# Weights split into high and low halves: two separate tiles, or one tile in which the halves alternate

## The chip, the core and the metric

One core of one Trainium2 chip runs the whole program. The metric is device time in microseconds, the median of three runs. The profile is of one further execution.

## The reference

A streaming encoder trunk of two layers with D = 2048 and 288 tokens: 256 of a prompt and 32 of a sample stream, which share all weights. Every token goes through the same weight products; the mixers in between work on chunks.

```
layer 0:  x += out_ab( retention(h) || gated linear attention(h) )      h = rmsnorm(x)
          x += convffn(rmsnorm(x))
layer 1:  x += out_att( chunked band attention with bias(h) )           h = rmsnorm(x)
          x += convffn(rmsnorm(x))
y = rmsnorm(x)

convffn(h):  g, u = split(h @ w_up);  act = silu(causal conv3(g) + b) * u;  return act @ w_down      (D_FF = 5632)
```

All inputs, weights and outputs are float32. Beside y the program returns the recurrent states, the new keys and values, and the last gate rows of the convolutions.

## The kernel before, in words

Activations lie transposed: 128 features on the partitions, 288 tokens along the row. A 128-row piece of the model dimension is one tile row of 288 float32, that is 1152 bytes. Every weight product is a sum of matmuls of a 128x128 weight block (stationary) with such a row (moving). To keep float32 accuracy with the float32r form of the matmul, both operands are split into a high half, rounded to float32r, and a low half, the rest; each block is multiplied three times: high by high, high by low, low by high (`passes`, L83 to L85). The three matmuls each load their weights anew, so the high weights are loaded twice running.

`project` (L65) makes one output tile of 128 features: it walks over 16 or 22 blocks in chunks of up to 8 (`WCH`). For each chunk `weights` (L54) issues one DMA of 512 KB on SP's queue into `w` (four buffers), lets ACT cast it into `wh` (L61) and DVE subtract into `wl` (L62), three buffers each. The tile framework places the waits: a cast waits until PE has read the buffer that it reuses.

The moving operands are constants for the whole program: `xh`, `xl` (the normed input of a layer) and `bh`, `bl` (the input of an output projection or of the down product). Before the change the two halves of piece k lie side by side in one tile `x{k}` of 2304 bytes, and likewise in `b`. The further rows that the down product needs (k from 16 to 21) are tiles of the same form in the FFN's own pool (`ffn`, L290).

Stages in order: `start` computes the first products straight from a packed input `x_first`, in pieces given by `cuts` (L92), while the data arrives; `ab_mixer` runs eight heads in an order written out by `chain`; `out_proj` (L277) adds its products to the residual `x`, which is loaded anew from DRAM by four DMAs on SP's queue just ahead of it (L219, L220), because its place served as mixer storage until then; then FFN, attention, out_proj, FFN. SP's queue carries the weights in program order. POOL's queue carries small loads, states and outputs. Padding in some constant tiles (`ones`, `w2`, `x`) moves what is allocated behind them.

The functions that the diff touches follow.

Of the kernel before, what the change touches and what calls it, by code (L numbers as in the profile page):

```python
# [5 lines left out]
F32 = mybir.dt.float32  # L6
# [6 lines left out]
P = 128  # L13
# [24 lines left out]
class Trunk:  # L38
# [15 lines left out]
    def weights(self, src, n, lo=False):  # L54

        nc = self.nc
        w = self.wp.tile([P, WCH, P], F32, name="w", tag="w", bufs=4)[:, :n, :]
        h = self.wp.tile([P, WCH, P], F32R, name="wh", tag="wh", bufs=3)[:, :n, :]
        l = self.wp.tile([P, WCH, P], F32R, name="wl", tag="wl", bufs=3)[:, :n, :]
        nc.sync.dma_start(w, src)  # L60
        nc.scalar.copy(h, w)  # L61
        nc.vector.tensor_tensor(l, w, h.bitcast(F32), op=ALU.subtract)  # L62
        return h, l

    def project(self, src, xh, xl, nk, k0=0, chunks=None, part=None, ps=None):  # L65
# [21 lines left out]
    def first_products(self, src, xw, lo_h):  # L87


        nc = self.nc  # L90
        ps = [self.acc_ps.tile([P, 512], F32, name="acc", tag="acc")[:, :T] for _ in range(N_FIRST + 1)]
        cuts = (0, 1, 2, 3, 4, 6, 8, 10, 12, 14, 16)  # L92

        for _ in range(8):
            nc.tensor.matmul(self.mm()[:, :P], lhsT=self.ones, rhs=self.ones, start=True, stop=True)
        for c, (i, j) in enumerate(zip(cuts, cuts[1:])):
            n = j - i
            nc.sync.dma_start(xw[:, i:j, :], src[:, i:j, :])
            w = xw[:, i:j, T : T + N_FIRST * P].rearrange("p k (o m) -> p k o m", o=N_FIRST)
            wlo = xw[:, i:j, T + N_FIRST * P :]  # L100
            lo = lo_h[:, i:j, :]
            tile = lambda tag: self.wp.tile([P, WCH, P], F32R, name=tag, tag=tag, bufs=3)[
                :, : N_FIRST * n, :
            ].rearrange("p (k o) m -> p k o m", o=N_FIRST)
            h, l = tile("wh"), tile("wl")
            for k in range(i, j):
                self.gain_in(k, 0)
                if k == i:
                    if c:
                        nc.scalar.copy(h, w)  # L110
                    else:
                        nc.vector.tensor_copy(h, w)
                    nc.vector.tensor_tensor(l, w, h.bitcast(F32), op=ALU.subtract)
                    nc.gpsimd.tensor_copy(lo[:, :, :RANK], wlo)
                    nc.gpsimd.tensor_tensor(
                        lo[:, :, RANK : 2 * RANK], wlo, lo[:, :, :RANK].bitcast(F32), op=ALU.subtract
                    )
                first, last = k == 0, k == KD - 1
                at = k - i
                for o in range(N_FIRST):  # L120
                    nc.tensor.matmul(ps[o], lhsT=h[:, at, o, :], rhs=self.xh[k], start=first, stop=False)
                for o in range(N_FIRST):
                    nc.tensor.matmul(ps[o], lhsT=h[:, at, o, :], rhs=self.xl[k], start=False, stop=False)
                for o in range(N_FIRST):
                    nc.tensor.matmul(ps[o], lhsT=l[:, at, o, :], rhs=self.xh[k], start=False, stop=last)
                nc.tensor.matmul(ps[-1], lhsT=lo[:, at, :], rhs=self.xh[k], start=first, stop=False)
                nc.tensor.matmul(ps[-1], lhsT=lo[:, at, :], rhs=self.xl[k], start=False, stop=last)
        return ps
# [67 lines left out]
    def run(self, ctx):  # L196
        nc, a = self.nc, self.a

        ones = self.const("ones", [P, P + 32])
        self.ones, self.eps = ones[:, :P], ones[:, P : P + 1]  # L200
        xs = [self.const(f"x{k}", [P, 2, T], F32R) for k in range(KD)]
        self.xh, self.xl = [[x[:, i, :] for x in xs] for i in range(2)]
        b_all = self.const("b", [P, KD, 2, T], F32R)
        self.bh_all, self.bl_all = b_all[:, :, 0, :], b_all[:, :, 1, :]
        self.bh, self.bl = [[b_all[:, k, i, :] for k in range(KD)] for i in range(2)]
        self.R = self.const("R", [P, T])
        nc.vector.memset(self.ones, 1.0)
# [7 lines left out]
        with self.tc.tile_pool(name="x", bufs=1) as xp:  # L215

            x = xp.tile([P, KD * T + 16], F32, name="x", tag="x")[:, : KD * T].rearrange("p (k t) -> p k t", t=T)
            self.x = [x[:, k, :] for k in range(KD)]
            for k in range(0, KD, 4):  # L219
                nc.sync.dma_start(x[:, k : k + 4, :], a["xT"][:, k : k + 4, :])  # L220
            self.out_proj(a["w_out_ab"], 1, (WCH, 0))
            with self.tc.tile_pool(name="f0", bufs=2) as pool:
# [27 lines left out]
    def start(self, pool):  # L250
# [14 lines left out]

        self.w2 = self.const("w2", [P, 512 + 224])[: 2 * RANK + 1, :512]
        nc.sync.dma_start(self.w2, a["w2"])
# [8 lines left out]

    def out_proj(self, w, n, chunks):  # L277

        for m in range(KD):
            if m < len(self.started):  # L280
                ps = self.project(w[m], self.bh, self.bl, KD, chunks=chunks, part=1, ps=self.started[m])
            else:
                ps = self.project(w[m], self.bh, self.bl, KD, chunks=chunks)
            self.nc.vector.tensor_tensor(self.x[m], self.x[m], ps, op=ALU.add)
            self.norm_in(m, n)
        self.norm_stat()

    def ffn(self, pool, layer, n, x_all):
        nc, a = self.nc, self.a
        bs = [self._one(pool, f"b{k}", [P, 2, T], None, F32R) for k in range(KD, HALF)]  # L290
        bh, bl = [old + [b[:, i, :] for b in bs] for i, old in ((0, self.bh), (1, self.bl))]
        convp = self._one(pool, "convp", [P, NF, 4], a["convp"][:, layer])
# [74 lines left out]
    def head_out(self, pool, o, gates, hd, g):  # L367

        nc = self.nc
        sq = pool.tile([P, TP], F32, name="hsq", tag="hsq", bufs=1)  # L370
        sq2 = pool.tile([P, TP], F32, name="hsq2", tag="hsq2", bufs=1)
        nc.scalar.activation(sq, o[0], AF.Square)
# [94 lines left out]
    def ab_mixer(self, pool, k0, q0, v0, lo_ps, second):  # L467
# [38 lines left out]
        def ret(hd):  # L506
            if hd == 0:
                late["cos"], late["sin"] = one("cosR", [P, T], a["cos"]), one("sinR", [P, T], a["sin"])
                for t in late.values():
                    nc.gpsimd.tensor_tensor(t, t, self.R, op=ALU.mult)  # L510
# [16 lines left out]
    def gla_head(self, pool, hd, w, sums, masks, eyem, hg, s4, sts, first):  # L527
# [13 lines left out]
        z = [gate(0)] if first else []  # L541
        st = pool.tile([P, 256], F32, name="gst", tag="gst", bufs=GRP)
        nc.gpsimd.dma_start(st, a["state_gla"][hd])
        sts.append(st)

# [163 lines left out]
    def ret_head(self, pool, hd, w, cosR, sinR, kdec, hg, s4, sts, aside):  # L709
        nc, a = self.nc, self.a  # L710
        dec = pool.tile([P, 384], F32, name="dec", tag="dec")
        nc.gpsimd.dma_start(dec, a["dec"][hd])
        st = pool.tile([P, 2, 256], F32, name="rst", tag="rst", bufs=GRP)
        nc.gpsimd.dma_start(st, a["state_ret"][hd])
        sts.append(st.rearrange("p j v -> p (j v)"))

# [179 lines left out]
    def att_sample(self, pool, g, kept, v4, bd):  # L896
# [15 lines left out]
        s = pool.tile([P, T], F32, name="as4", tag="as4")  # L912
        own = pool.tile([P, GRP, TS], F32, name="own4", tag="own4")
        mx = pool.tile([P, 1], F32, name="mx4", tag="mx4")
# [22 lines left out]
        for i in range(2):  # L937
            for c, (_, _, vc) in zip(quarter, kept):
                nc.tensor.matmul(
                    po[c], lhsT=pT[:, 1 + i, c], rhs=vc[:, i, :], start=False, stop=i == 1, skip_group_check=True  # L940
                )
        o = pool.tile([P, P], F32, name="ao4", tag="ao4")
        nc.vector.tensor_scalar(o, po, sm, None, op0=ALU.mult)
# [141 lines left out]
```

## Time and profile before

| what | value |
| --- | --- |
| median of 3 runs | 2677.33 us (2676.45 to 2679.82) |
| profiled execution, its own time | 2679.3 us |
| its span, first to last instruction | 2677.2 us |
| PE, DVE, ACT, POOL busy | 99%, 58%, 42%, 5% |
| matmuls | 20079 |
| mean DMA rate | 167 GB/s |

The span is what the trace covers; the 2.1 us beside it lie outside the first and last instruction. PE is the matmul side of TensorE, PEld its weight loads, which overlap the matmuls. A matmul's duration overlaps the next one's, so durations don't add up to time; distances between starts do.

### The profile page before, as it was taken

The numbers are of one execution on the slowest core, as the hardware profiler recorded it, in microseconds if no ns is written. First come the engines' busy times: TensorE is split into PE (matmuls) and PEld (weight loads), VectorE is DVE, ScalarE is ACT, GpSimd is POOL, SyncE is SP. The second block draws the span as 40 slices with busy tenths as digits, with TensorE's granted clock in tenths as the row PEclk, the third lists the DMA queues.
The fourth block names the chain that finished last, engine by engine and source line by source line (L and its number), as shares of the span: only waits on it lengthen the run. The fifth ranks groups of instructions, "written<-read, shape, count | busy, mean of one in ns | idle before, by whom it ended". The sixth has DMA issues, their size and how long they took to land. (4 is left out here: it accounts for less than half of the span.)

```text
span 2677.2 us, 48712 instructions
## 1 busy us (share of the span) xinstructions
PE 2661.0 (99%) x20079; PEld 2642.5 (99%) x20079; DVE 1560.8 (58%) x2593; ACT 1126.1 (42%) x1511; POOL 132.8 (5%) x459
## 2 busy tenths in 40 slices
PE   9999999999999999999999999999999999999998
PEld 9999999999999999999999999999999999999998
DVE  8665555566664456665555555556666545666544
ACT  7564445443333333334444443444333333333443
POOL 3000000000000000000021110000000000000000
PEclk9999999999999999999999999999999999999999
DMA  6444445555555555555565565555555555555554
GB/s 230 151 138 156 157 157 193 167 164 166 166 166 164 167 168 167 165 168 160 166 213 179 178 183 166 158 166 165 166 166 166 163 167 168 166 166 166 165 166 131
DMA packets 127227, 448.27 MB, mean 167 GB/s; under 512 B 16059, under 2 KB 16379, under 8 KB 127004
## 3 DMA queue, kind: packets, MB, share of 16 engines
q1 hardware_dynamic: 119852, 426.83, 51.5%
q0 software_dynamic: 7008, 18.29, 2.2%
q8 instruction: 157, 2.57, 0.4%
q14 instruction: 66, 0.54, 0.1%
q10 hardware_dynamic: 144, 0.04, 0.0%
HBM read 434.69 MB, written 10.40 MB: 166 GB/s over the span
## 5 line engine op out<-in xcount | busy, mean ns | idle before, releaser
L61 ACT CAST wh<-w 128x1024 fp32r<-128x1024 f32 (+1 forms) x812 | 839.2, 1034 | 1461.0 <-PE acc L84 1210.8
L62 DVE TENSOR_TENSOR wl<-w,wh 128x1024 fp32r<-128x1024 f32 (+1 forms) x812 | 976.4, 1203 | 738.4 <-ACT wh L61 737.4
L83 PE MATMUL acc<-x,wh 128*128 128x288 f32 x4432 | 1314.6, 297 | 0.0
L84 PE MATMUL acc<-x,wh 128*128 128x288 f32 x4432 | 1311.8, 296 | 0.0
L85 PE MATMUL acc<-x,wl 128*128 128x288 f32 x4432 | 1308.4, 295 | 0.0
L85 PEld LDWEIGHTS acc<-x,wl 128*128 128x128 f32 x4432 | 839.5, 189 | 0.3
L83 PEld LDWEIGHTS acc<-x,wh 128*128 128x128 f32 x4432 | 833.0, 188 | 1.6 <-issue 1.1
L84 PEld LDWEIGHTS acc<-x,wh 128*128 128x128 f32 x4432 | 833.3, 188 | 0.3
L83 PE MATMUL acc<-b,wh 128*128 128x288 f32 x1920 | 567.4, 296 | 0.5 <-ACT wh L61 0.5
L85 PE MATMUL acc<-b,wl 128*128 128x288 f32 x1920 | 566.2, 295 | 0.7 <-DVE wl L62 0.7
L84 PE MATMUL acc<-b,wh 128*128 128x288 f32 x1920 | 566.9, 295 | 0.0
L85 PEld LDWEIGHTS acc<-b,wl 128*128 128x128 f32 x1920 | 363.2, 189 | 1.2 <-DVE wl L62 1.0
L83 PEld LDWEIGHTS acc<-b,wh 128*128 128x128 f32 x1920 | 360.6, 188 | 1.3 <-ACT wh L61 1.1
L84 PEld LDWEIGHTS acc<-b,wh 128*128 128x128 f32 x1920 | 360.8, 188 | 0.1
L316 DVE SCALAR_TENSOR_TENSOR gc<-gp,convp,gc 128x290 f32<-128x290 f32 x176 | 91.2, 518 | 3.1
L322 DVE TENSOR_TENSOR v<-acc,R 128x288 f32<-128x288 f32 x88 | 40.3, 458 | 88.6 <-PE acc L85 88.6
L307 DVE TENSOR_TENSOR gp<-acc,R 128x256 f32<-128x256 f32 x88 | 37.4, 425 | 90.3 <-PE acc L85 90.1
L309 POOL COPY conv_out<-gp 128x2 f32<-128x2 f32 x88 | 16.4, 187 | 1309.3 <-DVE gp L307 1309.3
L147 ACT CAST b<-v 128x288 fp32r<-128x288 f32 x88 | 38.2, 434 | 16.1 <-DVE v L324 16.1
L323 DVE TENSOR_TENSOR v<-v,sg 128x256 f32<-128x256 f32 x88 | 37.4, 426 | 10.6 <-DVE v L322 1.8
L314 DVE TENSOR_SCALAR gc<-gp,convp 128x290 f32<-128x290 f32 x88 | 38.0, 431 | 9.4
L332 DVE TENSOR_TENSOR x<-x,acc 128x288 f32<-128x288 f32 x64 | 29.1, 454 | 19.2 <-PE acc L85 19.2
(301 smaller groups left out, 1140.1 us busy)
## 6 DMA issues: line engine op xcount, KB each, us to landing
w<-in_w_ffn_up SPq DMA_DIRECT2D x352, 512.0 KB, 3.7
w<-in_w_ffn_down SPq DMA_DIRECT2D x128, 512.0 KB, 3.7
w<-in_w_in SPq DMA_DIRECT2D x108, 512.0 KB, 3.8
w<-in_w_qkv SPq DMA_DIRECT2D x96, 512.0 KB, 3.8
w<-in_w_ffn_down SPq DMA_DIRECT2D x64, 384.0 KB, 3.2
w<-in_w_out_ab SPq DMA_DIRECT2D x32, 512.0 KB, 3.9
w<-in_w_out_att SPq DMA_DIRECT2D x32, 512.0 KB, 3.7
xw<-in_x_first SPq DMA_DIRECT2D x6, 560.0 KB, 7.9
```

Source lines behind the costliest of these rows:

```text
L61: nc.scalar.copy(h, w)
L62: nc.vector.tensor_tensor(l, w, h.bitcast(F32), op=ALU.subtract)
L83: nc.tensor.matmul(ps, lhsT=h, rhs=xh, start=first, stop=False)
L84: nc.tensor.matmul(ps, lhsT=h, rhs=xl, start=False, stop=False)
L85: nc.tensor.matmul(ps, lhsT=l, rhs=xh, start=False, stop=last)
L147: self.nc.scalar.copy(h, v)
L307: nc.vector.tensor_tensor(gp[:, 2 : TP + 2], g[:, :TP], self.R[:, :TP], op=ALU.mult)
L314: nc.vector.tensor_scalar(gc, gp[:, 0:W], cw[:, 0:1], cw[:, 3:4], op0=ALU.mult, op1=ALU.add)
L316: nc.vector.scalar_tensor_tensor(gc, gp[:, w : w + W], cw[:, w : w + 1], gc, op0=ALU.mult, op1=ALU.add)
L322: nc.vector.tensor_tensor(v, u, self.R, op=ALU.mult)
L323: nc.vector.tensor_tensor(v[:, :TP], v[:, :TP], s[:, :TP], op=ALU.mult)
L332: nc.vector.tensor_tensor(self.x[m], self.x[m], ps, op=ALU.add)
```

## The change

Four things change. The high and low half of a weight chunk go into one tile `whl` of twice the size in which they alternate element by element: `h` and `l` are views with a step of two elements, written so by ACT and DVE and read so by the weight loads. The moving operands become rows of 1152 bytes each, first all high rows, then all low rows, placed first in the constant pool. The residual is loaded in eight pieces of two rows on POOL's queue from within `out_proj`; from the third on, a one-element copy from a row that has just been added comes first, so that a piece goes out after that addition. The first products take the first eight rows one by one. Further, some tiles of the mixer and of attention share buffers or have fewer, and a padding shrinks.

```
 def weights(...):
-        h = self.wp.tile([P, WCH, P], F32R, name="wh", tag="wh", bufs=3)[:, :n, :]
-        l = self.wp.tile([P, WCH, P], F32R, name="wl", tag="wl", bufs=3)[:, :n, :]
+        h, l = self.split_weights(n)
...
+    def split_weights(self, n):
+        t = self.wp.tile([P, WCH, P, 2], F32R, name="whl", tag="whl", bufs=3)
+        return t[:, :n, :, 0], t[:, :n, :, 1]
...
-        cuts = (0, 1, 2, 3, 4, 6, 8, 10, 12, 14, 16)
+        cuts = (0, 1, 2, 3, 4, 5, 6, 7, 8, 10, 12, 14, 16)
...
-            tile = lambda tag: self.wp.tile([P, WCH, P], F32R, name=tag, tag=tag, bufs=3)[
-                :, : N_FIRST * n, :
-            ].rearrange("p (k o) m -> p k o m", o=N_FIRST)
-            h, l = tile("wh"), tile("wl")
+            h, l = [x.rearrange("p (k o) m -> p k o m", o=N_FIRST) for x in self.split_weights(N_FIRST * n)]
...
+        self.xh, self.xl = [[self.const(f"x{h}{k}", [P, T], F32R) for k in range(KD)] for h in "hl"]
+        self.bh_all, self.bl_all = [self.const(f"b{h}", [P, KD, T], F32R) for h in "hl"]
+        self.bh, self.bl = [[b[:, k, :] for k in range(KD)] for b in (self.bh_all, self.bl_all)]
+        self.R = self.const("R", [P, T])
         ones = self.const("ones", [P, P + 32])
-        xs = [self.const(f"x{k}", [P, 2, T], F32R) for k in range(KD)]
-        self.xh, self.xl = [[x[:, i, :] for x in xs] for i in range(2)]
-        b_all = self.const("b", [P, KD, 2, T], F32R)
-        self.bh_all, self.bl_all = b_all[:, :, 0, :], b_all[:, :, 1, :]
-        self.bh, self.bl = [[b_all[:, k, i, :] for k in range(KD)] for i in range(2)]
-        self.R = self.const("R", [P, T])
...
-            for k in range(0, KD, 4):
-                nc.sync.dma_start(x[:, k : k + 4, :], a["xT"][:, k : k + 4, :])
-            self.out_proj(a["w_out_ab"], 1, (WCH, 0))
+            self.out_proj(a["w_out_ab"], 1, (WCH, 0), x)
...
-        self.w2 = self.const("w2", [P, 512 + 224])[: 2 * RANK + 1, :512]
+        self.w2 = self.const("w2", [P, 512 + 32])[: 2 * RANK + 1, :512]
...
 def out_proj(self, w, n, chunks, load=None):
+        def piece(k, n):
+            nc.gpsimd.dma_start(load[:, k : k + n, :], self.a["xT"][:, k : k + n, :])
+        if load is not None:
+            piece(0, 2)
+            piece(2, 2)
         for m in range(KD):
...
+            k = 2 * m + 4
+            if load is not None and k < KD:
+                nc.vector.tensor_copy(load[:, k : k + 2, :1], load[:, m : m + 1, :1].to_broadcast([P, 2, 1]))
+                piece(k, 2)
             self.norm_in(m, n)
...
 def ffn(...):
-        bs = [self._one(pool, f"b{k}", [P, 2, T], None, F32R) for k in range(KD, HALF)]
-        bh, bl = [old + [b[:, i, :] for b in bs] for i, old in ((0, self.bh), (1, self.bl))]
+        bh, bl = [
+            old + [self._one(pool, f"b{h}{k}", [P, T], None, F32R) for k in range(KD, HALF)]
+            for h, old in (("h", self.bh), ("l", self.bl))
+        ]
...
-        sq2 = pool.tile([P, TP], F32, name="hsq2", tag="hsq2", bufs=1)
+        sq2 = pool.tile([P, TP], F32, name="on", tag="on", bufs=2)
...
-                late["cos"], late["sin"] = one("cosR", [P, T], a["cos"]), one("sinR", [P, T], a["sin"])
-                for t in late.values():
+                late["cos"], late["sin"] = [pool.tile([P, T], F32, name="sp", tag="sp", bufs=2) for _ in range(2)]
+                for x, t in late.items():
+                    nc.gpsimd.dma_start(t, a[x])
...
-        st = pool.tile([P, 256], F32, name="gst", tag="gst", bufs=GRP)
+        st = pool.tile([P, 512], F32, name="st", tag="st", bufs=GRP) if hd % 2 == 0 else None
+        sts += [st[:, :256], st[:, 256:]] if hd % 2 == 0 else []
...
-        st = pool.tile([P, 2, 256], F32, name="rst", tag="rst", bufs=GRP)
+        st = pool.tile([P, 512], F32, name="st", tag="st", bufs=GRP)
...
-        own = pool.tile([P, GRP, TS], F32, name="own4", tag="own4")
+        own = pool.tile([P, GRP, TS], F32, name="own4", tag="own4", bufs=1)
...
-        o = pool.tile([P, P], F32, name="ao4", tag="ao4")
+        o = pool.tile([P, P], F32, name="ao4", tag="ao4", bufs=1)
```

## Rows read from the trace of the kernel before

**Rows 1.** The page: engines' busy time, and the clock by slice

```profile
PE 2661.0 (99%) x20079; PEld 2642.5 (99%) x20079; DVE 1560.8 (58%) x2593; ACT 1126.1 (42%) x1511; POOL 132.8 (5%) x459
PEclk9999999999999999999999999999999999999999
```

**Rows 2.** Waits: who waited for whom, us in total, times, longest

```profile
PE mm L95 <- DVE ones L208: 1.1, 1, 1.1
...
ACT wh L61 <- PE acc L84: 1210.8, 633, 3.8
...
SPq L220 <- DMA out_ret_out<-rst: 6.4, 3, 5.3
```

**Rows 3.** The page's groups by line: busy us, mean ns of one

```profile
L61 ACT CAST wh<-w 128x1024 fp32r<-128x1024 f32 (+1 forms) x812 | 839.2, 1034 | 1461.0 <-PE acc L84 1210.8
L62 DVE TENSOR_TENSOR wl<-w,wh 128x1024 fp32r<-128x1024 f32 (+1 forms) x812 | 976.4, 1203 | 738.4 <-ACT wh L61 737.4
L83 PE MATMUL acc<-x,wh 128*128 128x288 f32 x4432 | 1314.6, 297 | 0.0
...
L85 PE MATMUL acc<-b,wl 128*128 128x288 f32 x1920 | 566.2, 295 | 0.7 <-DVE wl L62 0.7
```

**Rows 4.** Windows in both FFNs: length, busy time and counts, clock, DMA share, GB/s

```profile
840.00:960.00 120.00, 120.00 (x907) 120.00 (x906) 53.80 (x56) 40.26 (x41) 0.00 (x0) 1.00 0.60 169
980.00:1240.00 260.00, 260.00 (x1963) 260.00 (x1962) 162.63 (x266) 102.03 (x123) 9.89 (x58) 1.00 0.54 166
```

**Rows 5.** Timeline of PE, twelve steps of the float32r form: start, duration

```profile
1099.77 0.29 PE L83 MATMUL acc<-x,wh 128*128 128x288 f32 x1
...
1101.36 0.30 PE L83 MATMUL acc<-x,wh 128*128 128x288 f32 x1
```

**Rows 6.** Timeline of PE, float32 forms and transposes in attention

```profile
1501.42 0.59 PE L889 MATMUL mm<-ap,avt 128*128 128x256 f32 x2
1501.85 0.38 PE L890 MATMUL mm<-ap,avt 128*128 128x128 f32 x2
...
1502.29 0.60 PE L853 MATMUL mm<-ak,aq 128*128 128x256 f32 x2
1502.73 0.27 PE L857 MATMUL mm<-ident,av 128*128 128x128 f32 x1
1502.84 0.27 PE L858 MATMUL mm<-ident,av 128*128 128x128 f32 x1
```

**Rows 7.** Weight loads by form: ns min, median, max

```profile
L907 PEld LDWEIGHTS mm<-ak,aq x32: 106/108/110, 1458.8 to 1717.3; 128*32 128x32 f32 x32
...
L853 PEld LDWEIGHTS mm<-ak,aq x32: 191/192/192, 1395.0 to 1716.5; 128*128 128x128 f32 x32
```

**Rows 8.** DVE in the GLA levels, all seven together: ns min, median, max

```profile
L617 DVE TENSOR_TENSOR E<-sums x28: 267/282/286, 38.4 to 151.1; 128x128 f32<-128x128 f32 x28
...
L625 DVE TENSOR_TENSOR qk<-k,E x28: 278/292/294, 45.0 to 185.0; 128x128 f32<-128x128 f32 x28
```

**Rows 9.** Timeline around the reload of the residual

```profile
442.21 2.33 POOL L808 DMA_DIRECT2D out_ret_out<-rst  x4 [11.85 <-DVE rst L807]
448.38 1.85 SPq L220 DMA_DIRECT2D x<-in_xT  x4
450.34 9.16 SPq L60 DMA_DIRECT2D w<-in_w_out_ab  x4
452.80 0.82 DVE L284 TENSOR_TENSOR x<-x,acc 128x288 f32<-128x288 f32 x2 [3.84 <-DMA x<-in_xT]
455.72 1.98 ACT L61 CAST wh<-w 128x1024 fp32r<-128x1024 f32 x2
456.80 0.40 PE L83 MATMUL acc<-b,wh 128*128 128x288 f32 x1 [0.50 <-ACT wh L61]
```

**Rows 10.** Timeline of the start

```profile
0.74 5.25 SPq L98 DMA_DIRECT2D xw<-in_x_first  x10
...
9.25 0.53 PE L121 MATMUL acc<-x,wh 128*128 128x288 f32 x2 [0.55 <-ACT wh L110]
```

More of the change, by code (lines that the diff above doesn't have):

```diff
@@ L275, in start, with out_proj @@
         return k0, q0, v0, lo_ps, second
-    def out_proj(self, w, n, chunks):
+    def out_proj(self, w, n, chunks, load=None):
+        nc = self.nc
+        def piece(k, n):
[3 more added lines that the diff above has]
+            piece(2, 2)
         for m in range(KD):
@@ L283, in out_proj @@
                 ps = self.project(w[m], self.bh, self.bl, KD, chunks=chunks)
-            self.nc.vector.tensor_tensor(self.x[m], self.x[m], ps, op=ALU.add)
+            nc.vector.tensor_tensor(self.x[m], self.x[m], ps, op=ALU.add)
+            k = 2 * m + 4
+            if load is not None and k < KD:
+                nc.vector.tensor_copy(load[:, k : k + 2, :1], load[:, m : m + 1, :1].to_broadcast([P, 2, 1]))
+                piece(k, 2)
             self.norm_in(m, n)
@@ L541, in gla_head @@
         z = [gate(0)] if first else []
-        st = pool.tile([P, 256], F32, name="gst", tag="gst", bufs=GRP)
-        nc.gpsimd.dma_start(st, a["state_gla"][hd])
-        sts.append(st)
+        st = pool.tile([P, 512], F32, name="st", tag="st", bufs=GRP) if hd % 2 == 0 else None
+        sts += [st[:, :256], st[:, 256:]] if hd % 2 == 0 else []
+        nc.gpsimd.dma_start(sts[hd], a["state_gla"][hd])
         E = pool.tile([P, 9, TP], F32, name="E", tag="E", bufs=1)
@@ L712, in ret_head @@
         nc.gpsimd.dma_start(dec, a["dec"][hd])
-        st = pool.tile([P, 2, 256], F32, name="rst", tag="rst", bufs=GRP)
-        nc.gpsimd.dma_start(st, a["state_ret"][hd])
-        sts.append(st.rearrange("p j v -> p (j v)"))
+        st = pool.tile([P, 512], F32, name="st", tag="st", bufs=GRP)
+        nc.gpsimd.dma_start(st.rearrange("p (j v) -> p j v", j=2), a["state_ret"][hd])
+        sts.append(st)
         def rope(base, name):
```

## Prediction, written before the change was run

> **What bounds the kernel now.** I read the page first: TensorE is busy 2661.0 of 2677.2 us, with 20,079 matmuls and as many weight loads, and its granted clock is at the full level in every slice; DVE is at 58%, ACT 42%, POOL 5% [rows 1]. The reader should see that no other engine can set the time as things stand. The waits come next: TensorE's own list holds seven waits, none over 1.1 us [rows 2]. The span less PE's busy time is 16.2 us [rows 1]; the waits can be at most 7.7 of it, seven times the longest; the rest is mainly the end, where the final norm and the output run without PE. A schedule change can win one or two microseconds; anything larger has to change how long one matmul takes.
>
> So the third view is the distance from one matmul to the next. The "mean ns of one", 295 to 297 [rows 3], overlaps the next matmul and is not it. In undisturbed FFN stretches 1963 matmuls take 260 us and 907 take 120 us [rows 4]: 132.4 ns. The timeline shows the same step, twelve matmuls in 1.59 us [rows 5]. The long windows hold up products (x moves), the short one down products (b moves); they agree, though DMA's share is 0.54 in one and 0.60 in the other and DVE is busy 63 and 45% of them: the step is TensorE's own, and does not depend on which row of the moving tiles is read.
>
> Is 132.5 ns the floor? Two nearest rows say no. (a) The f32 form with 256 columns: two at 1501.42, next at 1501.85, so 215 ns each; the pair at 1502.29 is followed at 1502.73, 220 ns [rows 6]. At 2.4 GHz, two clocks per column are 213.3 ns, so what is not columns is 2 to 6 ns. One clock per column for 288 columns is 120 ns; with the same 2 to 6 ns that is 122 to 126. (b) Weight loads alone: the two transposes start 110 ns apart (1502.73, 1502.84) with a 128-column load each [rows 6]. Neither stream alone needs 132.5; together they cost about 10 ns more than the slower one. In (a) the same 128-column load runs beside a moving read at half the rate, and the excess is absent. My reading, which the trace suggests and does not prove, is that the weight load and the full-rate moving read get in each other's way.
>
> **The interleaved weights.** Each load now steps 8 bytes per column rather than 4. Loads of 32 columns take 108 ns and of 128 columns 191 [rows 7]: 0.86 ns per column. Contiguous weights therefore advance at 4/0.86 = 4.6 bytes/ns in a partition, the moving row at 4/0.417 = 9.6. At 8 bytes per column the load advances at 9.3 bytes/ns, nearly the pace of the moving row. Two streams of different pace sweep past each other within every matmul and must meet; two streams of one pace keep their distance, so they meet hardly ever or all the time. By the tile sizes in order of allocation, moving rows start at multiples of 128 bytes and weights 64 bytes past one, before and after; a constant distance of 64 is the best guess for "hardly ever". No row shows a strided load, so the step is bounded from both sides: 120 ns (columns alone) below, and above, a load that needs twice as long per column, 128 x 1.72 = 220 ns, plus the 3 ns by which a transpose's step exceeds its columns. I take 123 ns, near the lower of the two f32 sequences in (a).
>
> The count is (4432 + 1920) x 3 from the page [rows 3], 48 more by the same lines into the mm tile, and 128 in the first products: 19,232. The sum is 19,232 x (132.5 - 123) = 183 us. The page TensorE: Matmul & The Clock Gate of the Trainium skill (section Back-to-back issue gap) gives columns/2.4 + 2.5 ns for an isolated stream; by that estimate the step would be 122.5 ns and the gain 192 us, but the measured 132.5 ns disagrees with it for this kernel as it stands.
>
> **The writers of these weights.** DVE writes at a step of two elements occur already: the innermost level of the GLA products reads and writes single elements two apart, and all seven levels lie within 267 to 286 and 278 to 294 ns for 128 elements [rows 8]. So the subtraction is taken at today's 1203 ns [rows 3]. No ACT row writes at such a step: between nothing and a doubling of 1034 ns. Doubled, ACT goes from 1126 to 1965 us busy, still inside the span. What covers it: the cast waits for PE 633 times, 1211 us in all [rows 2], that is, it starts when a buffer comes free, two chunks (2 x 24 x 123 ns = 5.9 us) before its weights are due, and needs 1.03 + 1.20 us, or 3.3 doubled. I take zero. One tile for both halves means the cast may now wait for the last L85 instead of L84, 0.13 us later, and if the tracking is by whole tiles the first product waits for the subtraction; both lie inside that cover. It is gone only at the start, where PE already waited 0.5 us for ACT.
>
> **The moving rows.** The rows stay 1152 contiguous bytes at multiples of 128, in another order. The x rows and the b rows give the same step today [rows 4]: zero.
>
> **The residual.** Today four loads stand in SP's queue ahead of out_proj's weights: issued from 448.38 after waits of 6.4 us on the output DMA of the states [rows 2], and the next weight load goes out at 450.34 [rows 9]. ACT then casts at 455.72, PE waits 0.50 us for it at 456.80 [rows 9] and once 0.7 for DVE [rows 3]. Moved to POOL's queue, they no longer hold the weights: up to 1.2 us back, of which I count 1. What is late next: POOL's queue, where the pieces stand behind the four state outputs (issues from 442.21, 2.33 us) and ahead of convp and hist. x[0] is added at 452.80 today after 3.84 us of waiting for this load; PE starts its fifth output tile at 456.80 [rows 9] and has four accumulators, so piece 0 may come up to 4 us later before PE stands. Six later pieces each follow an addition and are needed at least four output tiles, 25 us, after; their six one-element copies are DVE work of at most 0.2 us each beside a 58% load.
>
> **The start and the shared buffers.** Twelve pieces instead of ten: two more issues at some 0.5 us each (ten take 5.25) put the loads behind them 1 us later, while the 0.55 us wait at 9.25 for a two-row piece [rows 10] may go: zero, within 1. The shared tiles (cos and sin, both kinds of state, hsq2, own4, ao4) add waits on POOL and DVE in front of transfers that are wanted a head later; cover is the 42% in which DVE is idle. Should one reach PE, it costs what the waits of [rows 2] cost, about 1 us. Zero.
>
> **Sum.** The profiled execution took 2679.3 us (span 2677.2, 2.1 around it), 2 above the median. 2679.3 - 183 - 1 = 2495; against the median, 2493. I say 2493.
>
> **The rivals.**
> 1. *Part of the excess goes*, as when the streams still meet at the turn from one matmul to the next: step 127.7, half of 9.5, so 91 us less: about 2586.
> 2. *Nothing changes.* The excess is a fixed price of this matmul form and not a meeting of streams: 2676. For it: the step is the same in every place. Against it: the f32 form lacks it. The TensorE page (Part 2, step 1) states this rule: weights and moving operand have independent read ports, so loading the next weights takes nothing from the running matmul. By that rule the time would stay; the trace bears it out only in the f32 rows, at half the rate.
> 3. *The streams keep the wrong distance* and meet all the time (slower). If half the path meets today and costs 12.5 ns over 120, all of it would cost 25: a step of 145, 240 us more: 2918. It decides as soon as the average meeting exceeds today's. For it: nothing in the trace fixes where the two reads stand when they run. Against it: the 64 bytes.
> 4. *The strided load runs at half rate* (slower): 223 ns, 90.5 x 19,232 = 1740 us more: 4420. For it: no strided load in the trace. Against it: DVE's two-element step at the full rate. Advanced Engine Details and Errata (SBUF Cachelines) asks for two hits per 16-byte line for full speed, which an 8-byte step of 4-byte elements just meets; the DVE rows agree, no run here shows it for TensorE.
> 5. *Strided writes double on DVE too*: 1560.8 + 976 = 2537 us busy. If the matmul step falls, DVE becomes the bound at about 2560; if not, queueing costs some tens of us.
>
> **How the numbers follow.** Forecast 0.42; rivals 1 and 5 with a falling step 0.18; rival 2 0.12; small losses without a gain (5, or a late queue) 0.06; rival 3 0.17; rival 4 0.05. Faster by over 0.2% (5 us, about what a measurement of this kernel can tell): 0.60; within: 0.12; slower: 0.28. The forecast's own range is 2445 (step 120.5) to 2555 (126.2). The range of 8 in 10 takes in rivals 1, 2, 5 and the mild end of 3: 2445 to 2760.
>
> **What would show it.** Right: windows of 260 us with some 2110 matmuls, the same ACT and DVE durations, no wait on SP for the state outputs, PE's list of waits as short as now. Wrong: the same 1963 (rival 2), or fewer; a longer weight load (rival 4); PE waiting on L61 or L62 throughout (rival 5). A moved step with x or b alone would say that the rows' places matter.

## The result, and the profile after

The changed kernel takes 2694.65 us (2694.24 to 2695.58, 4 runs) beside 2677.50 for the kernel before: a ratio of 1.0063, interval 1.0046 to 1.0081. It is slower by 17 us, where 2493 us, a gain of 184, was forecast.

The page of the changed kernel, its first lines and the costliest groups by line (weights are now the tile whl, moving rows xh, xl, bh, bl; the three products stand in L86 to L88, the cast in L60, the subtraction in L61):

```profile
span 2693.8 us, 48702 instructions
...
PE 2677.0 (99%) x20079; PEld 2659.2 (99%) x20079; DVE 1576.6 (59%) x2601; ACT 1185.9 (44%) x1513; POOL 137.7 (5%) x471
...
PEclk9999999999999999999999999999999999999999
...
L60 ACT CAST whl<-w 128x1024 fp32r<-128x1024 f32 (+1 forms) x812 | 906.8, 1117 | 1434.6 <-PE acc L88 1144.9
L61 DVE TENSOR_TENSOR whl<-w,whl 128x1024 fp32r<-128x1024 f32 (+1 forms) x812 | 979.2, 1206 | 805.7 <-ACT whl L60 787.2
...
L87 PEld LDWEIGHTS acc<-xl,whl 128*128 128x128 f32 x4432 | 873.0, 197 | 0.4
```

TensorE is still the bound and still at its full clock; the span less its busy time is 16.8 us, where [rows 1] had 16.2. Nearly the whole loss lies inside PE's busy time (2661.0 to 2677.0) with the same 20,079 matmuls. A load of these products takes 197 ns (188 before), the cast 1117 ns (1034 in [rows 3]), the subtraction 1206 (1203). The same two windows as [rows 4]:

```profile
840.00:960.00 120.00, 120.00 (x903) 120.00 (x902) 52.11 (x54) 42.67 (x41) 0.00 (x0) 1.00 0.57 166
980.00:1240.00 260.00, 260.00 (x1953) 260.00 (x1952) 166.32 (x266) 106.22 (x121) 10.37 (x61) 1.00 0.53 164
```

Ten matmuls fewer in 260 us, four fewer in 120, the clock at 1.00. A matmul counts in a window if any part of it lies there, which adds two or three to every count, so the step itself is better read between far starts. In the timeline of PE, after:

```profile
999.71 0.30 PE L86 MATMUL acc<-xh,whl 128*128 128x288 f32 x1
...
1159.71 0.30 PE L86 MATMUL acc<-xh,whl 128*128 128x288 f32 x1
```

and before:

```profile
999.79 0.30 PE L85 MATMUL acc<-x,wl 128*128 128x288 f32 x1
...
1158.91 0.29 PE L85 MATMUL acc<-x,wl 128*128 128x288 f32 x1
```

Both pairs are 1200 matmuls apart: 160.00 us and 159.12 us, or 133.33 and 132.60 ns each. At 2.4 GHz 133.33 ns are 320.0 clocks. The step grew by 0.74 ns (0.73 from these rows at 10 ns resolution), and 0.74 x 19,232 = 14.2 us of the 16.6 by which the span grew. The rest is small change in the mixers and at out_proj, where PE's longest wait now lies (the first line in its list of waits; 0.7 us at the same place in [rows 3]):

```profile
PE acc L88 <- DVE whl L61: 1.8, 1, 1.8
```

### The profile page after: what moved, and what is told of

It reads as the page before. It is cut to its first block, busy times and chain, and to the rows that moved or that the text cites. A ratio compares the mean times of both kernels' runs of the same rounds, so it can differ in the third digit from the quotient of the medians.

```text
span 2693.8 us, 48702 instructions
## 1 busy us (share of the span) xinstructions
PE 2677.0 (99%) x20079; PEld 2659.2 (99%) x20079; DVE 1576.6 (59%) x2601; ACT 1185.9 (44%) x1513; POOL 137.7 (5%) x471
## 4 chain that ended last, share of the span: by engine, by line
PE 96%; issue 3%; ACT 0%; DVE 0%; DMA 0%; POOL 0%; DVEq 0%; POOLq 0%; ACTq 0%
PE acc L86 31%; PE acc L87 30%; PE acc L88 30%; PE mm L586 0%; PE mm L900 0%; PE mm L864 0%; ACT whl L60 0%; PE mm L773 0%; PE acc L121 0%; PE mm L404 0%; PE acc L123 0%; PE mm L652 0%; PE acc L125 0%; DVE y L356 0%; DMA out_ret_out<-st 0%
## 5 line engine op out<-in xcount | busy, mean ns | idle before, releaser
L60 ACT CAST whl<-w 128x1024 fp32r<-128x1024 f32 (+1 forms) x812 | 906.8, 1117 | 1434.6 <-PE acc L88 1144.9
L61 DVE TENSOR_TENSOR whl<-w,whl 128x1024 fp32r<-128x1024 f32 (+1 forms) x812 | 979.2, 1206 | 805.7 <-ACT whl L60 787.2
L86 PE MATMUL acc<-xh,whl 128*128 128x288 f32 x4432 | 1326.0, 299 | 0.0
L87 PE MATMUL acc<-xl,whl 128*128 128x288 f32 x4432 | 1319.5, 298 | 0.0
L88 PE MATMUL acc<-xh,whl 128*128 128x288 f32 x4432 | 1311.6, 296 | 0.0
L87 PEld LDWEIGHTS acc<-xl,whl 128*128 128x128 f32 x4432 | 873.0, 197 | 0.4
L86 PEld LDWEIGHTS acc<-xh,whl 128*128 128x128 f32 x4432 | 867.9, 196 | 1.6 <-issue 1.1
L88 PEld LDWEIGHTS acc<-xh,whl 128*128 128x128 f32 x4432 | 869.1, 196 | 0.4 <-issue 0.3
L86 PE MATMUL acc<-bh,whl 128*128 128x288 f32 x1920 | 571.5, 298 | 0.0
L87 PE MATMUL acc<-bl,whl 128*128 128x288 f32 x1920 | 571.3, 298 | 0.0
L88 PE MATMUL acc<-bh,whl 128*128 128x288 f32 x1920 | 567.8, 296 | 1.8 <-DVE whl L61 1.8
L88 PEld LDWEIGHTS acc<-bh,whl 128*128 128x128 f32 x1920 | 376.3, 196 | 2.1 <-DVE whl L61 2.1
L87 PEld LDWEIGHTS acc<-bl,whl 128*128 128x128 f32 x1920 | 377.7, 197 | 0.0
L86 PEld LDWEIGHTS acc<-bh,whl 128*128 128x128 f32 x1920 | 376.0, 196 | 0.7 <-issue 0.5
```

Of the source, the lines that this page charges most:

```text
L86: nc.tensor.matmul(ps, lhsT=h, rhs=xh, start=first, stop=False)
L87: nc.tensor.matmul(ps, lhsT=h, rhs=xl, start=False, stop=False)
L88: nc.tensor.matmul(ps, lhsT=l, rhs=xh, start=False, stop=last)
```

## The experiments

Times in us, medians; "before" is the kernel before on the same chip, and the runs lie on four chips. A step is the time from one matmul's start to the next.

| run | time | before | ratio (interval) | step in the FFNs, ns |
|---|---|---|---|---|
| alternation alone | 2695.18 | 2676.76 | 1.0067 (1.0054 to 1.0080) | 133.33 |
| separate rows alone | 2673.18 | 2676.76 | 0.9986 (0.9977 to 0.9995) | 132.2 to 132.3 |
| change, reload on SP | 2695.10, one run | 2676.76 | | 133.33 |
| rows, weights moved 64 bytes | 2692.16 | 2677.81 | 1.0053 (1.0039 to 1.0067) | 133.1 to 133.3 |
| change, contiguous weights | 2676.63 | 2678.73 | 0.9993 (0.9984 to 1.0002) | 132.2 to 132.3 |
| that, rows and weights at one distance | 2666.27 | 2678.73 | 0.9955 (0.9942 to 0.9967) | 131.67 |
| kernel before, weights moved 64 bytes | 2664.31, one run | 2677.81 | | 132.22 in the first, 131.11 in the second |
| the same, on another chip | 2657.62 | 2678.73 | 0.9932 (0.9919 to 0.9945) | 131.11 |
| change, contiguous weights, reload on SP | 2672.57 | 2676.82 | 0.9984 (0.9975 to 0.9993) | 132.2 to 132.3 |

**Alternation alone** (e1_alternate_only). The kernel before with the one function for the weights, which the first products use too, and nothing else of the change:

```diff
-        h = self.wp.tile([P, WCH, P], F32R, name="wh", tag="wh", bufs=3)[:, :n, :]
-        l = self.wp.tile([P, WCH, P], F32R, name="wl", tag="wl", bufs=3)[:, :n, :]
+        h, l = self.split_weights(n)
...
+    def split_weights(self, n):
+        t = self.wp.tile([P, WCH, P, 2], F32R, name="whl", tag="whl", bufs=3)
+        return t[:, :n, :, 0], t[:, :n, :, 1]
...
```

> Only the weights alternate; rows, residual and buffers as before. Theory A (the strided weight load makes the matmul step longer, 132.6 to 133.3 ns): the weight load takes 196 ns instead of 188, the step is about 133.3, the time about 2692, ratio 1.005. Theory B (the order of the moving rows does it): load 196 but step 132.6, time within 3 us of 2677, ratio 1.000 to 1.001. ACT's cast should be 1117 ns in both, since only the weights' layout touches it.

It took 2695.18, 18.4 above the kernel before. Its window, and that of the next run, in this order:

```profile
980.00:1240.00 260.00, 260.00 (x1952) 260.00 (x1952) 166.44 (x266) 106.44 (x122) 10.39 (x61) 1.00 0.52 164
```

```profile
980.00:1240.00 260.00, 260.00 (x1969) 260.00 (x1968) 162.05 (x264) 101.70 (x123) 9.80 (x58) 1.00 0.53 165
```

The alternation by itself gives the whole slower step and all of the lost time.

**Separate rows alone** (e2_rows_only). The kernel before with the tiles xh, xl, bh, bl of the change, weights as they were:

```diff
+        self.xh, self.xl = [[self.const(f"x{h}{k}", [P, T], F32R) for k in range(KD)] for h in "hl"]
...
-        xs = [self.const(f"x{k}", [P, 2, T], F32R) for k in range(KD)]
-        self.xh, self.xl = [[x[:, i, :] for x in xs] for i in range(2)]
...
```

> Only the moving rows are laid out anew; weights in two tiles as before. Theory A: load 188 ns, step 132.6, ratio 1.000. Theory B: step 133.3 with a load of 188, about 14 us more, ratio 1.005. If both matter only together, e1 and e2 both stay at 2677.

2673.18, a small gain of 3.6 us: six matmuls more in 260 us. In the change the gain is not to be seen; with alternating weights the step is 133.33 with either set of rows.

**The change with the reload on SP** (e3_reload_on_sp).

```diff
-            self.out_proj(a["w_out_ab"], 1, (WCH, 0), x)
+            for k in range(0, KD, 4):
+                nc.sync.dma_start(x[:, k : k + 4, :], a["xT"][:, k : k + 4, :])
+            self.out_proj(a["w_out_ab"], 1, (WCH, 0))
```

> The changed kernel with the residual loaded on SP's queue in four pieces again. The matmul step stays 133.3 under every theory. If the reload in pieces on POOL's queue costs the 1.5 to 2 us that out_proj after the mixer lost, this run is some 1 to 2 us shorter than the changed kernel (2693.8 of span) and the 1.8 us wait of PE for the subtraction is gone; if the alternating tile costs it, the span stays within 0.5 us and the wait stays.

2695.10 with the same step; the place of the reload is worth nothing that can be measured while the weights alternate.

**Streams of one matmul** (p1_streams, p2_places_and_widths, p3_columns_and_types). Ahead of the second FFN stand streams of 108 matmuls that read one fixed piece of weights and one fixed moving row out of the b tile into a tile that nobody reads; each matmul has its weight load, as in the kernel. They measure the form by itself, and their own time is no result. The function, shortened:

```python
def stream(name, n=288, m=128, step=1, w=16, mov=0, mstep=1, count=108):
    ps = self.mm_ps.tile([P, 512], F32, name=name, tag="mm")[:m, :n]
    lhs = flat[:, W + w : W + w + m * step : step]
    rhs = flat[:, MOV + mov : MOV + mov + n * mstep : mstep]
    for i in range(count):
        self.nc.tensor.matmul(ps, lhsT=lhs, rhs=rhs, start=i == 0, stop=i == count - 1)
```

Arguments are moving columns n, weight columns m, the steps in elements, and the places w of the weights and mov of the row in elements of four bytes.

> The kernel before with twenty streams of 108 float32r matmuls each ahead of the last FFN, which change one thing each: place of the weights (0, 16, 32, 64 bytes past a multiple of 128), their step (1, 2, 4, 8 elements), columns of weights (128, 64, 32), columns moved (256, 288, 384, 512), place and step of the moving row. Their products are not used; the outputs stay those of before. Theory M (weight load and moving read meet, the prediction's reading): 132.5 ns as the base, about 122 to 126 with 32 columns of weights, a dependence on the places at step 2, and 223 at 512 columns if the load costs 10 ns there too. Theory F (a fixed price per matmul of this form): columns/2.4 + 12.5 throughout, so 119, 132.5, 172.5 and 226 for 256, 288, 384, 512 columns, whatever the weights are. Theory P (price per moved column, 10%): 118, 132.5, 177, 236.

The timeline of PE, where each row is a stream; the step is the distance to the next row's start over the count. pstep and pstep2w read weights at a step of two elements, pn512s (step two) and pn512m (32 weight columns) have 512 moving columns, pmstep reads the moving row at a step of two, pbase is the form of the kernel before. The last line is a window of 10 us within the stream of 256 moving columns and 128 weight columns:

```profile
1883.95 14.56 PE L243 MATMUL pstep<-b 128*128 128x288 f32 x108
1898.35 14.56 PE L243 MATMUL pstep2w<-b 128*128 128x288 f32 x108
...
2048.66 25.36 PE L243 MATMUL pn512s<-b 128*128 128x512 f32 x108
2073.86 25.12 PE L243 MATMUL pn512m<-b 128*32 128x512 f32 x108
2098.82 43.43 PE L243 MATMUL pmov<-b 128*128 128x288 f32 x324
2142.08 27.96 PE L243 MATMUL pmstep<-b 128*128 128x288 f32 x108
2169.86 14.57 PE L243 MATMUL pbase<-b 128*128 128x288 f32 x108
2184.27 0.30 PE L85 MATMUL acc<-x,wl 128*128 128x288 f32 x1
...
1994.00:2004.00 10.00, 10.00 (x91) 10.00 (x90) 0.00 (x0) 0.00 (x0) 0.00 (x0) 1.00 0.01 2
```

Weights at a step of two: 14.40 / 108 = 133.33 ns; contiguous ones at the same place: 14.41, the same. With 512 columns the step is 25.20 / 108 = 233.3 ns, and with a quarter of the weight columns still 24.96 / 108 = 231.1. A moving row at a step of two nearly doubles the step: 27.78 / 108 = 257.2. The 256 columns take 113.3 ns (the window's 91 less some three at its edges) and 384 take 173.3, so none of the three theories foretells the series: M fails at 32 weight columns (130.0 where it has 122 to 126), F and P at 256 (119 and 118).

> Thirty more streams of 108 matmuls, products unused, outputs those of the kernel before. (1) The weights' place, 0 to 224 bytes in steps of 32 from the moving row's (modulo 256), contiguous: if places matter as the first streams say, 131.7 at 0, 133.3 at 32 and 64, and 131.7 at 192 again; if the first streams differed by chance of order, no pattern. (2) The same at a step of two elements, six places: if a load at that step always comes to the worst case, 133.3 in all six; if places still matter, some at 131.7. (3) Both moved together by 32, 64, 96 bytes: 131.7 if the distance alone counts. (4) Widths: if the price is one clock in eight columns and not one of the weights, the steps grow by 1.125 clocks a column (0.469 ns), with 32 columns of weights as with 128, less at most 5 ns.

From the second set: qae to qah are contiguous weights at 128, 160, 192 and 224 bytes; qba to qbf are weights at a step of two in six places; qda to qdd are contiguous weights with 128, 192, 240 and 264 moving columns; qea has 256 moving columns and 32 weight columns, and qeb's row gives its end:

```profile
1881.89 14.57 PE L243 MATMUL qae<-b 128*128 128x288 f32 x108
1896.30 14.38 PE L243 MATMUL qaf<-b 128*128 128x288 f32 x108
1910.52 14.44 PE L243 MATMUL qag<-b 128*128 128x288 f32 x108
1924.80 14.56 PE L243 MATMUL qah<-b 128*128 128x288 f32 x108
1939.20 14.56 PE L243 MATMUL qba<-b 128*128 128x288 f32 x108
...
2025.60 14.39 PE L243 MATMUL qca<-b 128*128 128x288 f32 x108
...
2068.26 12.17 PE L243 MATMUL qda<-b 128*128 128x128 f32 x108
2080.27 12.25 PE L243 MATMUL qdb<-b 128*128 128x192 f32 x108
2092.36 12.29 PE L243 MATMUL qdc<-b 128*128 128x240 f32 x108
2104.48 13.13 PE L243 MATMUL qdd<-b 128*128 128x264 f32 x108
...
2197.39 12.88 PE L243 MATMUL qea<-b 128*32 128x256 f32 x108
2210.11 13.61 PE L243 MATMUL qeb<-b 128*32 128x272 f32 x108
```

Contiguous weights give 14.22 / 108 = 131.7, 14.28 / 108 = 132.2 or 14.40 / 108 = 133.3 ns by their place (133.4 at 128 bytes, 14.41 / 108); alternating ones 133.3 in every place (1939.20 to 2025.60 is 86.40 us for six streams). With few columns the step does not fall under 12.01 / 108 = 111.2 to 112.2 ns: there the 128-column load sets the pace, as at the 110 ns of the transposes in [rows 6]. With 256 columns the large load gives the shorter step: 113.3 ns, against 12.72 / 108 = 117.8 with a quarter of the weight columns, though at another place.

> Streams once more, products unused. (1) 64 and 32 columns of weights at steps of 1, 2, 4 elements. If a load disturbs by the number of 16-byte lines that it touches, 64 columns at step 2 (32 lines, as many as 128 contiguous ones) come to 316 to 320 clocks like those, and 64 contiguous columns to fewer, near 314; if the step of two by itself locks to 320, 64 and 32 columns at step 2 come to 133.3 ns too. (2) bfloat16 for both operands: if the price of one clock in twelve columns belongs to rows of 4-byte elements, 288 columns take 120 to 123 ns and 512 take 213 to 217; if it belongs to every matmul, 130 and 231. (3) 128 columns at a step of 3 elements: between 133 and the 233 of step 4.

In the third set rf and rg have 32 contiguous weight columns at two places, rh 32 at a step of two; rk has 128 at a step of three; rl is the kernel's form at place 0; rm and rn have bfloat16 operands of 288 and 512 columns:

```profile
1898.68 14.32 PE L248 MATMUL rf<-b 128*32 128x288 f32 x108
1912.84 14.09 PE L248 MATMUL rg<-b 128*32 128x288 f32 x108
1926.76 14.28 PE L248 MATMUL rh<-b 128*32 128x288 f32 x108
...
1968.96 19.03 PE L248 MATMUL rk<-b 128*128 128x288 f32 x108
1987.82 14.38 PE L248 MATMUL rl<-b 128*128 128x288 f32 x108
...
2002.05 13.41 PE L248 MATMUL rm<-half 128*128 128x288 bf16 x108
2015.29 23.47 PE L248 MATMUL rn<-half 128*128 128x512 bf16 x108
2038.69 23.48 PE L248 MATMUL ro<-half 128*32 128x512 bf16 x108
```

With a load of 32 columns, which takes 108 ns instead of 188, the step is 14.16 / 108 = 131.1 and 13.92 / 108 = 128.9 ns, against 131.7 to 133.3 with 128 columns. A load of 64 alternating columns gives 131.1 to 133.2 by its place, so the single value of 133.3 belongs to 128 of them. bfloat16 takes 13.24 / 108 = 122.6 ns for 288 columns and 216.7 for 512. So most of the excess over one clock per column goes with the four-byte form and not with the size of its load: with a quarter of the load, 128.9 to 131.1 is 9 to 11 ns over 120 at 288 columns, and 231.1 is 17.8 over 213.3 at 512. Whether it lies in reading the row or in what the array does with it is not shown: bfloat16 changed both operands, and no stream runs without a load. That the load's place still moves the step, and that 256 columns take less with the larger load, shows that the two do bear on each other, by some 4 ns.

**Where the weights lie** (e4_rows_and_place, e5_pairs_and_place, e5b_pairs_and_place). From the first streams I had a rule for the distance between weights and rows, 0 or 128 bytes modulo 256, and tried it with both layouts of the rows. Sixteen elements more behind w2 move every weight tile by 64 bytes, and sixteen fewer behind x keep the rest in place:

```diff
-        self.w2 = self.const("w2", [P, 512 + 224])[: 2 * RANK + 1, :512]
+        self.w2 = self.const("w2", [P, 512 + 240])[: 2 * RANK + 1, :512]
...
-            x = xp.tile([P, KD * T + 16], F32, name="x", tag="x")[:, : KD * T].rearrange("p (k t) -> p k t", t=T)
+            x = xp.tile([P, KD * T], F32, name="x", tag="x")[:, : KD * T].rearrange("p (k t) -> p k t", t=T)
```

> The rows of the change with contiguous weights whose tiles start at a multiple of 128 bytes instead of 64 past one. If a distance of 0 or 128 bytes (modulo 256) is the good place, the step is 131.7 ns everywhere: 19,232 x 0.9 ns = 17 us less than before, about 2660, ratio 0.9935. If places don't matter in the kernel, 132.3 as with the rows alone, 2673.

> The kernel before with the weights' place moved alone, rows in pairs as before. Distances are 0 and 128 bytes modulo 256 here as well, so the step should be 131.7 too, and the time near 2660, if places are what counts; if the order of the rows gave the 3.6 us of the rows-only run, it is 2 to 4 us longer than the run with rows and place.

> The kernel before with the weights' place moved, once more and timed. If the step is fixed by the addresses and the order, its profile repeats 132.22 in the first FFN and 131.11 in the second and the time 2664, ratio 0.995. If the two levels come from chance at the start of a run, the levels differ and the times scatter by some 10 us.

With separate rows it gave 2692.16, the slow step; with the pairs of the kernel before, 2664.31 in one run and then, on another chip, 2657.62 (2656.88 to 2664.08). The rule failed in the first, and half of it was wrong by the streams themselves: the second set, which ran beside it, has 133.4 ns at 128 bytes. But the same distances, 0 and 128, gave a slow step with one layout of the rows and with the other 131.1, which no stream with these columns reached; so the distance alone does not settle the step of a kernel whose rows change with every matmul. The window of 260 us in the two profiled executions of the second:

```profile
980.00:1240.00 260.00, 260.00 (x1969) 260.00 (x1968) 162.11 (x263) 101.81 (x122) 9.79 (x58) 1.00 0.52 166
```

```profile
980.00:1240.00 260.00, 260.00 (x1986) 260.00 (x1985) 163.70 (x265) 103.07 (x125) 9.79 (x58) 1.00 0.54 167
```

One program, two steady steps: in the first FFN, where this window lies, 1969 matmuls in one execution and 1986 in the other, while the second FFN ran at 131.11 ns in both. The five times of the second chip alone fall into two groups that lie as far apart, three at 2656.9 to 2657.6 and two at 2663.7 to 2664.1, so it is no difference of the chips.

**The change with contiguous weights** (e6_change_contiguous), everything else of it kept:

```diff
-        t = self.wp.tile([P, WCH, P, 2], F32R, name="whl", tag="whl", bufs=3)
-        return t[:, :n, :, 0], t[:, :n, :, 1]
+        h, l = [self.wp.tile([P, WCH, P], F32R, name=x, tag=x, bufs=3) for x in ("wh", "wl")]
+        return h[:, :n, :], l[:, :n, :]
```

> The changed kernel with contiguous high and low tiles again, all else of the change kept: rows, residual in pieces, cuts, shared buffers. If the alternation is the whole loss, the step falls from 133.33 to the 132.32 of the rows-only run and the time to 2672 to 2675, ratio to before 0.998 to 0.999. If the residual or the shared buffers cost more than a microsecond, it is above 2676.

2676.63: giving up the alternation takes back 18.0 us of the changed kernel's time. It stays 3.5 above the rows alone though its step is theirs, and its trace shows a longer wait than they have, at the start of out_proj: the timeline on POOL, DVE, ACT and PE, and a window behind the wait (the third value from its end is the granted clock):

```profile
448.20 1.07 POOL L277 DMA_DIRECT2D x<-in_xT  x2 [4.39 <-DMA out_ret_out<-st]
454.16 0.82 DVE L287 TENSOR_TENSOR x<-x,acc 128x288 f32<-128x288 f32 x2 [5.95 <-DMA convp<-in_convp]
457.07 2.92 ACT L60 CAST wh<-w 128x1024 fp32r<-128x1024 f32 x3
458.15 0.61 PE L86 MATMUL acc<-bh,wh 128*128 128x288 f32 x1 [2.63 <-ACT wh L60]
...
461.00:464.40 3.40, 3.40 (x16) 3.40 (x16) 1.99 (x4) 0.76 (x2) 0.54 (x1) 0.50 0.82 258
```

**The same with the reload on SP** (e8_contiguous_reload_on_sp); the diff is that of the third run, on top of the one above.

> The change with contiguous weights and the residual's four loads back on SP's queue. Theory A (the reload in pieces costs PE about 4 us at out_proj, because the cast that it needs comes late behind the pieces): 2672.7 us, as with the rows alone (2673.2), and the wait of PE for ACT at the second projection falls from 2.63 us to under 1. Theory B (the reload is harmless; the 3.5 us between the two versions come from the other rearrangements, the shared tiles or the steady pattern): 2676.6 as with the pieces on POOL, with the step in the FFNs at 132.3 ns in either case.

2672.57, 4.1 under the version with the pieces and level with the rows alone. The same places in its trace, on SP, DVE, ACT and PE, and the same window:

```profile
447.20 1.98 SPq L217 DMA_DIRECT2D x<-in_xT  x4
451.30 0.82 DVE L289 TENSOR_TENSOR x<-x,acc 128x288 f32<-128x288 f32 x2 [3.42 <-DMA x<-in_xT]
454.21 1.98 ACT L60 CAST wh<-w 128x1024 fp32r<-128x1024 f32 x2
456.56 0.40 PE L88 MATMUL acc<-bh,wl 128*128 128x288 f32 x1 [0.73 <-DVE wl L61]
...
461.00:464.40 3.40, 3.40 (x28) 3.40 (x27) 3.33 (x6) 2.58 (x5) 0.00 (x0) 1.00 0.58 180
```

The pieces leave only 1.00 us later, but the first addition comes at 454.16 instead of 451.30, and the cast that PE wants at 457.07 instead of 454.21: 2.86 us both times. PE's waits for cast and subtraction here, 2.63 + 0.41 against 0.73, are 2.3 of the 4.1 us. The rest is the clock: after the 2.63 us in which PE stood, its granted clock lies at 0.50, the lower level of 1.2 GHz, and 19 matmuls from 459.81 to 464.13 start 240 ns apart instead of 132, about 1.9 us more; with the reload on SP it stays at 1.00. Laid matmul on matmul, the two traces part by 4.75 us at out_proj and by 0.35 at the start, and nowhere else by more than some hundredths.

**One distance** (e7_one_distance). The version with contiguous weights, 128 bytes behind each moving row, so that rows and weights all start at an odd multiple of 128:

```diff
-        self.xh, self.xl = [[self.const(f"x{h}{k}", [P, T], F32R) for k in range(KD)] for h in "hl"]
+        self.xh, self.xl = [[self.const(f"x{h}{k}", [P, T + 32], F32R)[:, :T] for k in range(KD)] for h in "hl"]
```

and so for bh, bl and the later b tiles, with the pads behind w2 (48) and x (32) to match.

> The same, with 128 bytes of space behind every moving row, so that all rows and all weights start 128 past a multiple of 256: distance 0 at every matmul. By the streams (131.67 at distance 0) the time is 19,232 x 0.65 ns = 12 us below the run without the space, about 2661. By the run with rows and place, in which the rule from the streams failed, it may as well be 133.3 and 2690: then a stream with fixed operands doesn't tell what a kernel gets whose operands change.

2666.27, with a step of 131.67 ns throughout the FFNs: the step of the streams at distance 0, as expected. The time is 5 us above the 2661 expected; it fell by 10.4 where 12 was forecast, from 2676.63 rather than 2673. Places matter, by a nanosecond or so a matmul.

## Why the prediction was wrong

**The step that failed is the floor: the term of 123 ns, and the question whether 132.5 ns is one.** The prediction took 122 to 126 from the f32 form and the transposes in [rows 6], and put the 10 ns above it down to weight load and moving row getting in each other's way. Its sentence that neither stream alone needs 132.5, and that together they cost about 10 ns more than the slower one, is what the streams refute: a 128-column load with few moving columns needs 111 to 112 ns, but float32r rows of 288 columns still take 128.9 to 131.1 with a quarter of the load, so 9 to 11 of the 12.6 ns of excess do not go with the load's size. The f32 form takes two clocks a column (215 ns for 256 in [rows 6]) and so shows nothing of this; a row of the same type and rate was wanted, and the trace of before had none. If the shortest of these steps is taken as the floor, a layout could win 3.7 ns at most (132.6 to 128.9), 71 us and not 183; the best version found gains 1.5 ns in the FFNs and 21 us in all.

**The alternation then went the other way.** The reasoning on one pace said nothing of which constant distance is a good one. The run with the alternation alone shows that it makes the whole loss; why 128 alternating columns always come to the upper value is not shown. With 128 weight columns, alternating weights come to 133.33 ns in two streams of the first set, in the six places of the second, and in the three kernels that have them; contiguous ones lie between 131.1 and 133.3, by place and by execution. The kernel before stood at 132.6, so it lost 0.74 ns, 14.2 us; against the change with contiguous weights and the reload on SP (132.3) the step differs by 1.0 ns, or 19 us over all of them, of the 22.5 between 2695.10 and 2672.57. Rival 3, a wrong distance, had the sign, with a step of 145 where 133.33 came. Rival 2, a fixed price of the form, was nearest in kind and size: most of the excess is that. The time lies in the range of 8 in 10 only by the mild end of rival 3, and that is luck: nothing in the sum led to it.

**The strided load** runs at nearly the full rate, 193 to 198 ns against 188, so rival 4 falls. **The writers** are as bounded: the cast grew by 83 ns of a possible 1034 and is covered as the prediction said, the subtraction by 3 ns; rival 5 falls. **The moving rows** were put at zero and gain 3.6 us alone; that x and b rows, laid out alike, gave one step said nothing of another order. **The start** held: the alignment of the two traces has the changed kernel's first product within 0.4 us of the former. **The shared buffers**, the twelve pieces at the start with them, held too: 2672.57 with all of them, 2673.18 with the rows alone.

**The residual** was put at 1 us won and is 4.1 us lost with contiguous weights. The failing step is the cover of up to 4 us, reckoned from PE's four accumulators. The cast that PE waits for in [rows 9] stands on ACT behind the activations of the norm, which follow the addition; that wait of 0.50 us said already that the cover was used up, and a later first piece goes straight to PE. With contiguous weights the longer wait also brings the lower clock, which the prediction did not reckon with. In the changed kernel itself the reload costs nothing that shows (2694.65 against 2695.10): PE waits there once, 1.84 us for the subtraction, at a granted clock of 1.00, where the run with the reload on SP waits 0.58 us for the cast and 0.72 for the subtraction. Why its wait is the shorter one was not tried.

**What stays open.** Why the float32r form costs about a twelfth more than its columns, and what picks among the steady steps of a layout. The distance rule from fixed operands failed in one kernel, held in the one with a single distance, and in a third the same program had two steps, so it is no rule yet.

## What to carry to other kernels

Take a floor from a row of the same type and rate as the form that is to become faster; an excess that a slower form lacks may belong to the faster form itself and to no conflict. To tell a conflict from a price, shrink one of the two parties: a quarter of the load left most of the excess, and a hundred matmuls on fixed operands showed it. Then look at what a wait leaves behind it: here the matmuls after a wait of 2.63 us ran at half the clock, which cost nearly as much again. And look behind an engine's wait at the order on the engine that it waits for: a transfer moved to another queue was late not for its own reader but for the cast queued behind it.

## What the runs showed of the hardware

- float32r matmuls cost 1.06 to 1.11 clocks per column at 2.4 GHz for rows at multiples of 32 bytes, wherever the load does not set the pace (256 columns: 113.3 ns with 128 weight columns, 117.8 with 32; 288: 128.9 to 133.3; 512: 231.1 and 233.3), bfloat16 1.02 at 288. The formula that the Trainium skill has for an isolated matmul (TensorE: Matmul & The Clock Gate, Back-to-back issue gap: columns/2.4 + 2.5 ns) gives 122.5 and 215.8 for 288 and 512 columns. The bfloat16 streams, in which every matmul has its load, agree with 122.6 and 216.7; for float32r at 288 columns the measured 128.9 to 133.3 decides.
- Weight loads of 128 columns: 188 ns contiguous, 193 to 198 at 8 bytes a column, 262 at 12 (step 18.86 / 108 = 174.6 ns). This agrees with the two hits per 16-byte line that the Trainium skill asks for (Advanced Engine Details and Errata, SBUF Cachelines). The moving row does not: at 8 bytes, with two hits a line, the step is 257.2 ns.
- After 2.63 us in which TensorE stood, its granted clock lies at 0.50, the level of 1.2 GHz (window 461.00:464.40), and matmuls of 288 columns start 240 ns apart; after a wait of 1.84 us in the changed kernel it stays at 1.00.
- Two profiled executions of one program differ by 6.9 us (spans 2662.2 and 2655.3) at the same clock, through the step of the first FFN (132.2 and 131.1 ns). With alternating weights five runs lie within 0.35 us; the fifteen runs of before beside them spread over 8.2.
